# Gated DeltaNet in a one-core decoder step: the 32x32 block inverses in one tile, the keys' norm in the delta rows' factor

## The chip, the core and the metric

One core of one Trainium2 chip. The metric is the device time of one execution in microseconds (us), from the first instruction to the last and the little that lies around them; lower is better. The engines are named as the profile names them: PE (matmuls), PEld (its weight loads), DVE, ACT, POOL, and SP, which here does nothing but issue DMAs.

## What is computed

One inference step of a two-layer decoder in fp32: a gated DeltaNet layer with a SwiGLU block, then a sparse-attention layer with a second SwiGLU block. It handles a prompt of 512 positions and, beside it, 8 sampled sequences of 4 positions each. Only the DeltaNet layer (the first 410 us) is touched. It has 8 heads of width 128, and the part that matters is this:

```python
k = l2norm(k.reshape(B_, T, DN_HEADS, DN_HEAD_K))
...
kk = jnp.einsum('bnhid,bnhjd->bnhij', kc, kc)
A = jnp.where(strict, bc[..., :, None] * dec * kk, 0.0)
L = A + jnp.eye(C, dtype=A.dtype)
wv = lax.linalg.triangular_solve(L, bc[..., None] * vc, ...)
wk = lax.linalg.triangular_solve(L, (bc * eG)[..., None] * kc, ...)
aqk = dec * jnp.einsum('bnhid,bnhjd->bnhij', qc, kc)
kdec = jnp.exp(G[..., -1:] - G)[..., None] * kc
...
def step(S, xc):
    U = wv_n - jnp.einsum('bhik,bhkv->bhiv', wk_n, S)
    O = jnp.einsum('bhik,bhkv->bhiv', qg_n, S) + jnp.einsum('bhij,bhjv->bhiv', aqk_n, U)
    S = gl_n[..., None, None] * S + jnp.einsum('bhik,bhiv->bhkv', kdec_n, U)
```

So per head and chunk a unit triangular matrix L is inverted, and the state S is carried from chunk to chunk through the delta rows U. The kernel uses chunks of 128, four a head.

## The kernel before, in words

Every projection is a `gemm` (L171): for each of 8 slices of the model width three fp32r matmuls, the high parts (L177), the activations' low part (L178) and the weights' low part (L179), into a PSUM bank named mm. The weights come by DMA into `wraw` (three buffers), ACT rounds them to `whi` (L158, 128x1024) and POOL or DVE takes the rest into `wlo` (L159). Per head there are four projections: k, q and v, each followed by a causal convolution on ACT, DVE and POOL (`qkv`, L444), and the gate z (`zgate`, L679).

The heads' other work is written as small generators, each with a letter:

- K, `keys` (L511): decay factors, the keys' squared norms (transpose on PE at L525, squares on ACT at L526 into `ssk`), the matrix B = strict part of L into `BB` (L535). After heads 3 and 7 the 32x32 diagonal blocks of four heads go to DRAM (`scr`).
- S, `keys_done` with `key_cols` (L567): the per-row factors, among them `rk` (one over the keys' norm), `brk` = beta times rk, `kd` and `irk`.
- D, `diag_inverse` (L580): the 64 diagonal blocks of a group of four heads are inverted by substitution, one block a partition. It runs twice (D0, D1). The 32 rows of a block are held in two halves of 16 rows (a = 0, 1), D and N, each half in a buffer of its own; for step l from 31 to 1 DVE forms a product (L595) and a difference (L597), for both halves as long as l is over 16. Then ACT writes the transposes (L600), and the two results go to DRAM (`scn`).
- I, `inverse` (L606): loads the blocks into `XX` and `XT` and builds the 128x128 inverse by block products on PE.
- Q, `queries` (L645): keys times queries into PSUM, scaled by `rk` and the decays into `aq` (L657).
- V, `values` (L694): transposed values and keys, `Vs` and `Kd` (L706).
- `head` (L709): the chain over four chunks. For each: the state's share is taken off the values (L722, L723), the inverse is applied (L725), ACT multiplies by `brk` (L727) to give U, then come the state's update (L728, L732) and the output (L729, L735).
- s, `sample_ks` (L758): loads a sampled head's state in two buffers (256 KB each) and multiplies it (L770). P, `sample`: the sampled sequences' state updates, with two more such loads a head.

Buffers of 128x512 fp32 for all of this come from one pool, `hb()` (L439), of 32; `diag_inverse` takes five of them. PSUM banks named ch serve K and the heads' chains.

The order of the work is written as text: `DN_START` runs through, then each of four `DN_PAIRS` weaves the chains of two heads with other generators and a list of inverses, then `DN_TAIL`. But each engine's own order is not that of the text: the framework's scheduler (the kernel is built with it switched on) places the instructions of every engine by its own timing, and chooses which freed buffer a new tile takes. Each engine then runs its list in order and waits at the head of it.

Of the kernel before, what the change touches and what calls it, by code (L numbers as in the profile page):

```python
# [17 lines left out]
D = 1024  # L18
# [21 lines left out]
ESPAN = 640  # L40
HB = 32
DN_START = "k0 K0 q1 k2 k1 K2 v1 k3 K1 z0 K3 S0 k4 q0 K4 Q0 v0 V1 D0 k5 q3 s0 v4 z1 Q1 V0 K5 s3 k6 k7 I0 q2 v3 I1 K6 Q3 K7 s2 Y0 Q2 s1 v2 V3"
# [69 lines left out]
class Net:  # L112
# [206 lines left out]
    def deltanet(self, up, ctx):  # L319
# [10 lines left out]
        dn = ctx.enter_context(tc.tile_pool(name="dn", bufs=1))  # L330
        gc, bc, Gc, nG, eG, neG, GL, kd, gl, ssk, sB, rk, irk, brk, sq2 = [
            dn.tile([128, NG], F32, name=n) for n in
            ("gc", "bc", "Gc", "nG", "eG", "neG", "GL", "kd", "gl", "ssk", "sB", "rk", "irk", "brk", "sq2")]
        hist = dn.tile([128, 24, 24], F32, name="hist")
# [232 lines left out]
        def key_cols(s):  # L567
            g = slice(s * 17, s * 17 + 17)
            V.tensor_scalar(irk[:, g], ssk[:, g], EPS, None, op0=OP.add)
            self.rsqrt(rk[:, g], irk[:, g])  # L570
            V.tensor_tensor(irk[:, g], irk[:, g], rk[:, g], op=OP.mult)
            V.tensor_tensor(brk[:, g], bc[:, g], rk[:, g], op=OP.mult)
            S.activation(gl[:, g], GL[:, g], AF.Exp)
            V.tensor_tensor(kd[:, g], GL[:, g], nG[:, g], op=OP.add)
            S.activation(kd[:, g], kd[:, g], AF.Exp)
            V.tensor_tensor(kd[:, g], kd[:, g], rk[:, g], op=OP.mult)
            S.activation(eG[:, g], Gc[:, g], AF.Exp)
            V.tensor_scalar(neG[:, g], eG[:, g], -1.0, None, op0=OP.mult)

        def diag_inverse(g):  # L580

            D, N = [[hb()[0:64].rearrange("p (j i) -> p j i", i=32) for _ in range(2)] for _ in range(2)]
            tmp = hb()[0:64]
            rows = scr[4 * g:4 * g + 4].rearrange("h c b j i -> (h c b) j i")
            for a in range(2):
                self.dma(D[a], rows[:, 16 * a:16 * a + 16])
                G.memset(N[a], 0.0)
                G.memset(N[a].rearrange("p j i -> p (j i)")[:, 16 * a:512:33], 1.0)
            for l in range(31, 0, -1):
                n = 32 - l  # L590
                row = N[l // 16][:, l % 16:l % 16 + 1, l:32]
                for a in range(2 if l > 16 else 1):
                    m = min(l - 16 * a, 16)
                    t = tmp[:, 256 * a:256 * a + m * n].rearrange("p (j i) -> p j i", i=n)
                    V.tensor_tensor(t, D[a][:, 0:m, l:l + 1].to_broadcast([64, m, n]), row.to_broadcast([64, m, n]),  # L595
                                    op=OP.mult)
                    V.tensor_tensor(N[a][:, 0:m, l:32], N[a][:, 0:m, l:32], t, op=OP.subtract)  # L597
            for a in range(2):
                for b in range(2):
                    S.copy(D[a][:, :, 16 * b:16 * b + 16], N[b][:, :, 16 * a:16 * a + 16].rearrange("p j i -> p i j"))  # L600
            out = scn[g] = self.dr.tile([2, 4, NC, 4, 32, 32], F32, name=f"scn{g}")
            for t, o in ((N, out[0]), (D, out[1])):
                for a in range(2):
                    self.dma(o.rearrange("h c b j i -> (h c b) j i")[:, 16 * a:16 * a + 16], t[a])

# [39 lines left out]
        def queries(h):  # L645
# [7 lines left out]
            for c in range(NC):  # L653
                cs = slice(c * 128, (c + 1) * 128)
                T.matmul(ps[:, cs], lhsT=kT[h][:, cs], rhs=qT[h][:, cs], start=True, stop=True)
            for c in range(NC):
                V.scalar_tensor_tensor(aq[h][:, c], ps[:, c * 128:(c + 1) * 128], rk[:, col(h, c)],  # L657
                                       aq[h][:, c], op0=OP.mult, op1=OP.mult)
            yield
# [10 lines left out]
        def sample_query(s):  # L670
            ps = self.bank("ch")
            q2s = wk.tile([128, 128], F32, name="q2s", bufs=1)
            G.tensor_tensor(q2s, stk(qS, s), stk(qS, s), op=OP.mult)
            T.matmul(ps[:, 128:129], lhsT=q2s, rhs=ones[:, 0:1], start=True, stop=True)
            V.tensor_scalar(sq2[:, scol(s)], ps[:, 128:129], EPS, EPS * 128, op0=OP.add, op1=OP.mult)
            T.matmul(ps[:, 0:128], lhsT=stk(kS, s), rhs=stk(qS, s), start=True, stop=True)
            V.scalar_tensor_tensor(decs[:, s], ps[:, 0:128], rk[:, scol(s)], decs[:, s], op0=OP.mult, op1=OP.mult)

# [30 lines left out]
        def head(h):  # L709
# [5 lines left out]
            for c in range(NC):  # L715
# [10 lines left out]
                U = DX[:, 0, h % 2]  # L726
                S.mul(U, pa[:, 128:256], brk[:, cl])  # L727
                T.matmul(pa[:, 256:384], lhsT=Kd[h][:, c], rhs=U, start=True, stop=True)  # L728
# [49 lines left out]
        def sample_u(s):  # L778
# [7 lines left out]
            U = wk.tile([128, 128], F32, name="Us", bufs=1)  # L786
            S.mul(U, ps[:, 128:256], brk[:, cl])
            T.matmul(ps[:, 256:384], lhsT=decs[:, s], rhs=U, start=True, stop=True)
# [1018 lines left out]
```

## Time and profile before

| | |
|---|---|
| median of 3 runs | 1661.45 us (1659.9 to 1662.36) |
| profiled execution, its own time | 1664.61 us |
| its span, first to last instruction | 1662.4 us |
| mean granted TensorE clock | 0.985 |
| busy: PE / DVE / ACT / POOL | 1596.2 / 1059.6 / 710.8 / 562.3 us |

The page gives each engine's busy time, the chain of work that ended last, and the costliest groups of instructions. The trace behind it answers narrower questions: what an engine waited for in a stretch, what a stretch held, the instructions of one engine in order of time. Times in those answers are us from the start of the span.

### The profile page before, as it was taken

What the parts mean: (1) busy time and instruction counts of PE and PEld (TensorE: products, weight loads), DVE (VectorE), ACT (ScalarE), POOL (GpSimd) and SP (SyncE); (2) the same over time, 40 slices, a digit from 0 to 9 for tenths busy, and PEclk for the clock granted to TensorE, in tenths of its full rate; (3) what the DMA queues carried; (4) which work ended last, traced back from release to release, by engine and by line L of the source; (5) the groups of instructions that cost most, each with busy time, mean ns of one, the idle gap of its engine ahead of it and who ended that gap; (6) DMA issues with size and microseconds to landing.
All of it is one profiled execution on the core that took longest, in us unless ns stands there. A gap on an engine that the chain in (4) does not pass through costs nothing.

```text
span 1662.4 us, 32746 instructions
## 1 busy us (share of the span) xinstructions
PE 1596.2 (96%) x12527; PEld 1526.5 (92%) x12527; DVE 1059.6 (64%) x2543; ACT 710.8 (43%) x1796; POOL 562.3 (34%) x861
## 2 busy tenths in 40 slices
PE   8998899998989999999999999999999999999997
PEld 6998788886989999999999899877999999999997
DVE  4878779477557753555456598677875553355533
ACT  5554554554322222233332488688843232132233
POOL 2776546424356621100045476565520000000000
PEclk9999999999999999999999999999999999999999
DMA  6233512256556635354343533523133332334232
GB/s 195 77 79 84 118 36 67 69 162 210 145 134 150 161 104 120 99 159 137 106 136 87 139 93 88 174 65 120 45 94 104 102 106 79 108 90 127 77 88 81
DMA packets 289068, 183.36 MB, mean 110 GB/s; under 512 B 25183, under 2 KB 271784, under 8 KB 288784
## 3 DMA queue, kind: packets, MB, share of 16 engines
q1 hardware_dynamic: 286352, 172.88, 38.0%
q0 software_dynamic: 2560, 8.39, 1.4%
q8 instruction: 98, 1.61, 0.4%
q14 instruction: 58, 0.48, 0.1%
HBM read 159.33 MB, written 26.90 MB: 112 GB/s over the span
## 4 chain that ended last, share of the span: by engine, by line
PE 76%; DVE 10%; POOL 4%; DMA 4%; ACT 3%; issue 3%; SPq 1%; POOLq 0%; DVEq 0%; ACTq 0%
PE mm L179 15%; PE mm L177 15%; PE mm L178 15%; PE aux L177 5%; PE aux L179 5%; PE aux L178 5%; PE po L1629 2%; PE aux L1656 2%; DVE hb L595 2%; DVE hb L597 1%; SPq L155 1%; DVE wlo L159 1%; PE mm L1566 1%; PE mm L818 1%; PE mm L1567 1%
## 5 line engine op out<-in xcount | busy, mean ns | idle before, releaser
L177 PE MATMUL mm<-uh,whi 128*128 128x288 f32 (+2 forms) x1824 | 531.5, 293 | 5.3 <-DVE hb L689 1.7
L178 PE MATMUL mm<-ul,whi 128*128 128x288 f32 (+2 forms) x1824 | 530.4, 292 | 0.0
L179 PE MATMUL mm<-uh,wlo 128*128 128x288 f32 (+2 forms) x1824 | 524.0, 292 | 4.8 <-DVE wlo L159 4.8
L158 ACT CAST whi<-wraw 128x1024 fp32r<-128x1024 f32 (+5 forms) x231 | 216.1, 936 | 525.6 <-PE mm L178 412.7
L177 PEld LDWEIGHTS mm<-uh,whi 128*128 128x128 f32 (+1 forms) x1824 | 344.2, 189 | 8.6 <-DVE hb L689 2.1
L179 PEld LDWEIGHTS mm<-uh,wlo 128*128 128x128 f32 (+1 forms) x1824 | 341.1, 189 | 6.9 <-DVE wlo L159 6.0
L178 PEld LDWEIGHTS mm<-ul,whi 128*128 128x128 f32 (+1 forms) x1824 | 344.6, 189 | 1.5 <-issue 0.4
L159 DVE TENSOR_TENSOR wlo<-wraw,whi 128x1024 fp32r<-128x1024 f32 (+5 forms) x207 | 233.1, 1126 | 108.6 <-ACT whi L158 107.1
L179 PE MATMUL aux<-uh,wlo 128*128 128x288 f32 (+1 forms) x704 | 202.1, 287 | 1.0 <-DVE wlo L159 0.9
L177 PE MATMUL aux<-uh,whi 128*128 128x288 f32 (+1 forms) x704 | 203.0, 288 | 0.0
L178 PE MATMUL aux<-ul,whi 128*128 128x288 f32 (+1 forms) x704 | 202.7, 288 | 0.0
L177 PE MATMUL mm<-hh,whi 128*128 128x256 f32 (+1 forms) x704 | 202.1, 289 | 0.0
L178 PE MATMUL mm<-hl,whi 128*128 128x256 f32 (+1 forms) x704 | 201.4, 288 | 0.0
L179 PE MATMUL mm<-hh,wlo 128*128 128x256 f32 (+1 forms) x704 | 196.5, 288 | 0.0
L184 POOL TENSOR_TENSOR ycol<-yvar,nhalf 128x2 f32<-128x2 f32 (+1 forms) x2 | 1.6, 776 | 398.0 <-DVE yvar L1704 398.0
L179 PEld LDWEIGHTS aux<-uh,wlo 128*128 128x128 f32 x704 | 132.4, 188 | 1.4 <-DVE wlo L159 1.4
L178 PEld LDWEIGHTS mm<-hl,whi 128*128 128x128 f32 x704 | 132.7, 188 | 0.0
L177 PEld LDWEIGHTS mm<-hh,whi 128*128 128x128 f32 x704 | 132.6, 188 | 0.0
L178 PEld LDWEIGHTS aux<-ul,whi 128*128 128x128 f32 x704 | 132.6, 188 | 0.0
L177 PEld LDWEIGHTS aux<-uh,whi 128*128 128x128 f32 x704 | 132.3, 188 | 0.2 <-issue 0.2
L179 PEld LDWEIGHTS mm<-hh,wlo 128*128 128x128 f32 x704 | 129.6, 188 | 0.0
L957 DVE SCALAR_TENSOR_TENSOR fup<-aux,rstd 128x256 f32<-128x256 f32 x88 | 38.7, 440 | 125.5 <-PE aux L179 125.5
(535 smaller groups left out, 2961.1 us busy)
## 6 DMA issues: line engine op xcount, KB each, us to landing
wraw<-in_ffn_w_in_dram SPq DMA_DIRECT2D x88, 512.0 KB
wraw<-in_dn_w_in_dram SPq DMA_DIRECT2D x32, 512.0 KB
wraw<-in_ffn_w_out_dram SPq DMA_DIRECT2D x32, 384.0 KB
wraw<-in_ffn_w_out_dram SPq DMA_DIRECT2D x32, 320.0 KB
hb<-in_state_dn_S_dram SPq DMA_DIRECT2D x32, 256.0 KB
wraw<-in_nsa_w_kv_dram SPq DMA_DIRECT2D x12, 512.0 KB
bskew<-bscr SPq DMA_DIRECT2D x16, 320.0 KB
x<-xd SPq DMA_DIRECT2D x16, 272.0 KB
```

The costliest lines, as they stand in the source:

```text
L155: return self.nc.sync.dma_start(out, in_)
L158: self.S.copy(hi, src)
L159: (self.G if pool_lo else self.V).tensor_tensor(lo, src, hi.bitcast(F32), op=OP.subtract)
L177: self.T.matmul(ps, lhsT=hi[:, k, :], rhs=uh[:, cs], start=first and k == 0, stop=False)
L178: self.T.matmul(ps, lhsT=hi[:, k, :], rhs=ul[:, cs], start=False, stop=False)
L179: self.T.matmul(ps, lhsT=lo[:, k, :], rhs=uh[:, cs], start=False, stop=last and k == kc - 1)
L595: V.tensor_tensor(t, D[a][:, 0:m, l:l + 1].to_broadcast([64, m, n]), row.to_broadcast([64, m, n]), op=OP.mult)
L597: V.tensor_tensor(N[a][:, 0:m, l:32], N[a][:, 0:m, l:32], t, op=OP.subtract)
L818: T.matmul(ps, lhsT=Kh, rhs=um[q], start=True, stop=True)
L957: V.scalar_tensor_tensor(up, pu, 0.5, rstd[:, cs], op0=OP.mult, op1=OP.mult)
L1629: T.matmul(self.po, lhsT=self.VT[ty][:, kb, g], rhs=m[:, i:i + 2].rearrange("p e q -> p (e q)"), start=False, stop=last and kb > k0 and m ...
L1656: T.transpose(ps[:, i * 128:(i + 1) * 128], P[2 * pr + e][ty][:, a:a + 128], ident)
```

## The change

Four things change in the DeltaNet layer, and the pool of `hb()` buffers goes from 32 to 28.

1. `diag_inverse` holds the block's 32 rows in one tile each, `inv` [64, 32, 32], two buffers of 4 KB a partition that are its own; from `hb()` it takes only the scratch `tmp`. Each of the 31 steps is one product (L588 in the new file) and one difference (L590). One ACT copy (L591) in place of four writes the transposes. One DMA instead of two loads the blocks, and two instead of four store them.
2. `brk` is gone and `kd` no longer holds `rk`; U is multiplied by `sB` (beta over the squared norm).
3. So `aq` needs no factor by row: one product over 128x512 (L646) in place of four over 128x128.
4. The same in the sampled sequences' code.

```diff
-HB = 32
+HB = 28
...
-            V.tensor_tensor(brk[:, g], bc[:, g], rk[:, g], op=OP.mult)
...
-            V.tensor_tensor(kd[:, g], kd[:, g], rk[:, g], op=OP.mult)
...
-            D, N = [[hb()[0:64].rearrange("p (j i) -> p j i", i=32) for _ in range(2)] for _ in range(2)]
+            D, N = [wk.tile([64, 32, 32], F32, name="inv", bufs=2) for _ in range(2)]
             tmp = hb()[0:64]
-            rows = scr[4 * g:4 * g + 4].rearrange("h c b j i -> (h c b) j i")
-            for a in range(2):
-                self.dma(D[a], rows[:, 16 * a:16 * a + 16])
-                G.memset(N[a], 0.0)
-                G.memset(N[a].rearrange("p j i -> p (j i)")[:, 16 * a:512:33], 1.0)
+            self.dma(D, scr[4 * g:4 * g + 4].rearrange("h c b j i -> (h c b) j i"))
+            G.memset(N, 0.0)
+            G.memset(N.rearrange("p j i -> p (j i)")[:, 0:1024:33], 1.0)
             for l in range(31, 0, -1):
                 n = 32 - l
-                row = N[l // 16][:, l % 16:l % 16 + 1, l:32]
-                for a in range(2 if l > 16 else 1):
-                    m = min(l - 16 * a, 16)
-                    t = tmp[:, 256 * a:256 * a + m * n].rearrange("p (j i) -> p j i", i=n)
-                    V.tensor_tensor(t, D[a][:, 0:m, l:l + 1].to_broadcast([64, m, n]), row.to_broadcast([64, m, n]),
-                                    op=OP.mult)
-                    V.tensor_tensor(N[a][:, 0:m, l:32], N[a][:, 0:m, l:32], t, op=OP.subtract)
-            for a in range(2):
-                for b in range(2):
-                    S.copy(D[a][:, :, 16 * b:16 * b + 16], N[b][:, :, 16 * a:16 * a + 16].rearrange("p j i -> p i j"))
+                t = tmp[:, 0:l * n].rearrange("p (j i) -> p j i", i=n)
+                V.tensor_tensor(t, D[:, 0:l, l:l + 1].to_broadcast([64, l, n]), N[:, l:l + 1, l:32].to_broadcast([64, l, n]),
+                                op=OP.mult)
+                V.tensor_tensor(N[:, 0:l, l:32], N[:, 0:l, l:32], t, op=OP.subtract)
+            S.copy(D, N.rearrange("p j i -> p i j"))
...
             for t, o in ((N, out[0]), (D, out[1])):
-                for a in range(2):
-                    self.dma(o.rearrange("h c b j i -> (h c b) j i")[:, 16 * a:16 * a + 16], t[a])
+                self.dma(o.rearrange("h c b j i -> (h c b) j i"), t)
...
-            for c in range(NC):
-                V.scalar_tensor_tensor(aq[h][:, c], ps[:, c * 128:(c + 1) * 128], rk[:, col(h, c)],
-                                       aq[h][:, c], op0=OP.mult, op1=OP.mult)
+            V.tensor_tensor(aq[h], by_chunk(ps), aq[h], op=OP.mult)
...
-                S.mul(U, pa[:, 128:256], brk[:, cl])
+                S.mul(U, pa[:, 128:256], sB[:, cl])
```

The order texts are the same, but the engines' lists are not: the scheduler lays out the DeltaNet layer anew on every engine (the lists agree again after it). Three places are shown.

ACT, where the transposes of D0 are written. Before (L600 is the copy; `whi_3104` is the gate weight of head 6; L526 squares a chunk of head 4's or 5's keys, which PE's L525 in the same bank follows):

```order
L456 COPY pre_2413<-mm_2416 128x256
L492 COPY cso_2402<-ch_2400 108x128
L158 CAST whi_3104<-wraw_3102 128x1024
L456 COPY pre_2413<-mm_2442 128x256
L458 COPY pre_2413<-mm_2442 128x8x4
L600 COPY hb_1579<-hb_1581 64x16x16
L600 COPY hb_1580<-hb_1581 64x16x16
L526 ACTIVATE junk2_112,ssk_95<-ch_2532 128x128
L478 ACTIVATE cth_2380<-cy_2379 128x544
```

And after the change (L591 is the one copy, `whi_3007` the same gate weight):

```order
L456 COPY pre_2364<-mm_2367 128x256
L591 COPY inv_1573<-inv_1574 64x1024
L492 COPY cso_2353<-ch_2351 108x128
L158 CAST whi_3007<-wraw_3005 128x1024
L456 COPY pre_2364<-mm_2393 128x256
L458 COPY pre_2364<-mm_2393 128x8x4
L526 ACTIVATE junk2_111,ssk_95<-ch_2483 128x128
L478 ACTIVATE cth_2331<-cy_2330 128x544
```

The copy, which needs all of D0, now stands ahead of the weights' cast and two copies out of PSUM; L526 is behind it in both.

SP, around the states of sampled heads 2 and 1 (`hb<-in_state_dn_S_dram`, two loads a head). Before:

```order
L155 DMA wraw_3469<-in_dn_w_in_dram 128x8x128
L155 DMA hb_2607<-in_state_dn_S_dram 128x4x128
L155 DMA hb_2613<-in_state_dn_S_dram 128x4x128
L155 DMA hb_2647<-in_state_dn_S_dram 128x4x128
L155 DMA hb_2653<-in_state_dn_S_dram 128x4x128
L155 DMA XT_115<-scn0_1686 32x8x32
...
L155 DMA scr_411<-BB_116 32x16x32 x4
L155 DMA hb_2768<-scr_411 64x512
L155 DMA hb_2769<-scr_411 64x512
```

After:

```order
L155 DMA wraw_3369<-in_dn_w_in_dram 128x8x128
L155 DMA XT_114<-scn0_1642 32x8x32
...
L155 DMA scr_410<-BB_115 32x16x32 x4
L155 DMA inv_2713<-scr_410 64x1024
L155 DMA hb_2555<-in_state_dn_S_dram 128x4x128
L155 DMA hb_2561<-in_state_dn_S_dram 128x4x128
L155 DMA hb_2592<-in_state_dn_S_dram 128x4x128
L155 DMA hb_2598<-in_state_dn_S_dram 128x4x128
L155 DMA out_p_dn_S_dram<-DX_116 128x128 x2
```

The four loads have moved behind the stores and the load of the second group's blocks. Their buffers have changed as well: before, they were those that D0 had given up; now the first takes the buffer of head 0's keys, the second that of its `Vs`, the third that of head 1's keys, and the fourth the first's again.

PE, the chains of heads 0 and 1. Before, from the middle of them (`ch<-DX` and `ch<-hb,XX` are the chains; mm_3181 is the projection q of head 4; L770 stood 10 rows further up):

```order
L724 MATMUL ch_2921<-DX_117,hb_644 128x128
L725 MATMUL ch_2921<-hb_1562,XX_114 128x128
L722 MATMUL ch_2957<-DX_117,hb_529 128x128
L177 MATMUL mm_3181<-uh_134,whi_3174 128x256
L178 MATMUL mm_3181<-ul_135,whi_3174 128x256
L179 MATMUL mm_3181<-uh_134,wlo_3175 128x256
...
L724 MATMUL ch_2957<-DX_117,hb_1349 128x128
L699 MATMUL aux_2900<-ct_69,hb_2663 128x128 x4
L728 MATMUL ch_2921<-DX_117,hb_1563 128x128
```

After (L710, L712, L713, L716 and L717 are what L722, L724, L725, L728 and L729 were; L758 is what L770 was):

```order
L717 MATMUL ch_2874<-DX_116,hb_1095 128x128
L712 MATMUL ch_2899<-DX_116,hb_1346 128x128
L713 MATMUL ch_2899<-hb_1986,XX_113 128x128
L710 MATMUL ch_2912<-DX_116,hb_809 128x128
L758 MATMUL aux_2554<-hb_2555,km_112 64x128 x4
...
L717 MATMUL ch_2912<-DX_116,hb_1095 128x128
L549 MATMUL ch_2973<-kS_102 128x128
L758 MATMUL aux_2591<-hb_2592,km_112 64x128 x4
L758 MATMUL aux_2591<-hb_2598,km_112 64x128 x4
L177 MATMUL mm_3084<-uh_133,whi_3077 128x256
```

In the new list no projection stands between the first matmul of the two chains and the last L758; in the old one q of head 4 and z of head 5 began among them, 18 rows before the chains' third chunk was done. As many projections stand ahead of the chains in both.

## Rows read from the trace of the kernel before

**Rows 1.** The page: busy time by engine, and the chain that ended last.

```profile
PE 1596.2 (96%) x12527; PEld 1526.5 (92%) x12527; DVE 1059.6 (64%) x2543; ACT 710.8 (43%) x1796; POOL 562.3 (34%) x861
...
PE 76%; DVE 10%; POOL 4%; DMA 4%; ACT 3%; issue 3%; SPq 1%; POOLq 0%; DVEq 0%; ACTq 0%
```

**Rows 2.** Waits of PE, 100 to 410 us: total us, times, longest us.

```profile
PE ch L525 <- ACT junk L526: 9.5, 3, 4.6
...
PE aux L621 <- DMA XT<-scn: 1.7, 1, 1.7
```

**Rows 3.** Stretches: us, busy PE, PEld, DVE, ACT, POOL, granted clock, DMA share, GB/s.

```profile
142.40:149.20 6.80, 4.56 (x18) 4.27 (x19) 5.70 (x23) 4.16 (x12) 0.69 (x5) 0.50 0.25 71
183.30:186.70 3.40, 3.40 (x17) 3.40 (x16) 2.84 (x5) 0.92 (x5) 2.64 (x5) 0.50 0.58 115
202.00:214.00 12.00, 12.00 (x105) 9.19 (x106) 8.43 (x32) 6.89 (x21) 1.49 (x6) 1.00 0.37 84
```

**Rows 4.** The groups of DVE: line, tiles, count, busy us, mean ns, idle before.

```profile
L595 DVE TENSOR_TENSOR hb<-hb 64x112 f32<-64x112 f32 (+19 forms) x92 | 37.9, 436 | 1.8 <-POOL hb L588 0.6
L597 DVE TENSOR_TENSOR hb<-hb 64x112 f32<-64x112 f32 (+19 forms) x92 | 31.6, 365 | 0.6
L657 DVE SCALAR_TENSOR_TENSOR hb<-aux,rk,hb 128x128 f32<-128x128 f32 x32 | 9.0, 340 | 8.3 <-PE aux L655 8.2
...
L706 DVE TENSOR_TENSOR hb<-aux,kd 128x512 f32<-128x512 f32 x8 | 5.5, 681 | 2.3 <-PE aux L705 2.2
```

**Rows 5.** DVE in order of time, D0: start us, us; x2 is both halves.

```profile
128.67 0.47 DVE L595 TENSOR_TENSOR hb<-hb 64x96 f32<-64x96 f32 x2
129.07 0.44 DVE L597 TENSOR_TENSOR hb<-hb 64x96 f32<-64x96 f32 x2
129.54 0.45 DVE L595 TENSOR_TENSOR hb<-hb 64x112 f32<-64x112 f32 x2
...
147.55 0.48 DVE L595 TENSOR_TENSOR hb<-hb 64x240 f32<-64x240 f32 x2
147.98 0.48 DVE L597 TENSOR_TENSOR hb<-hb 64x240 f32<-64x240 f32 x2
148.50 0.42 DVE L595 TENSOR_TENSOR hb<-hb 64x256 f32<-64x256 f32 x1
148.95 0.42 DVE L597 TENSOR_TENSOR hb<-hb 64x256 f32<-64x256 f32 x1
149.41 0.42 DVE L595 TENSOR_TENSOR hb<-hb 64x255 f32<-64x255 f32 x1
...
174.22 0.31 DVE L597 TENSOR_TENSOR hb<-hb 64x156 f32<-64x156 f32 x1
```

**Rows 6.** POOL in order of time, 134 to 142 us.

```profile
134.42 2.77 POOL L451 COPY pre<-hist 128x24 f32<-128x24 f32 x1
137.14 4.17 POOL L477 TENSOR_TENSOR cy<-cy,cts 128x32 f32<-128x32 f32 x1
...
141.71 0.25 POOL L477 TENSOR_TENSOR cy<-cy,cts 128x32 f32<-128x32 f32 x1
```

**Rows 7.** ACT in order of time, 142 and 173 to 182 us; brackets: idle before.

```profile
142.65 0.66 ACT L478 ACTIVATE cth<-cy 128x544 f32<-128x544 f32 x1 [6.37 <-POOL cy L477]
...
173.84 1.05 ACT L158 CAST whi<-wraw 128x1024 fp32r<-128x1024 f32 x1
174.80 0.37 ACT L456 COPY pre<-mm 128x256 f32<-128x256 f32 x1
...
181.00 1.17 ACT L600 COPY hb<-hb 64x256 f32<-64x256 f32 x2 [5.74 <-DVE hb L597]
```

**Rows 8.** PE in order of time: two waits in the chains of heads 6 and 7.

```profile
379.38 0.49 PE L728 MATMUL ch<-DX,hb 128*128 128x128 f32 x2 [0.43 <-ACT DX L727]
...
382.49 0.49 PE L724 MATMUL ch<-DX,hb 128*128 128x128 f32 x2 [0.44 <-DVE hb L723]
```

**Rows 9.** The chain that ended last, a DMA of 285 to 293 us.

```profile
290.62 1.91 DMA XT<-scn
```

More of the change, by code (lines that the diff above doesn't have):

```diff
@@ L330, in deltanet @@
         dn = ctx.enter_context(tc.tile_pool(name="dn", bufs=1))
-        gc, bc, Gc, nG, eG, neG, GL, kd, gl, ssk, sB, rk, irk, brk, sq2 = [
+        gc, bc, Gc, nG, eG, neG, GL, kd, gl, ssk, sB, rk, irk, sq2 = [
             dn.tile([128, NG], F32, name=n) for n in
-            ("gc", "bc", "Gc", "nG", "eG", "neG", "GL", "kd", "gl", "ssk", "sB", "rk", "irk", "brk", "sq2")]
+            ("gc", "bc", "Gc", "nG", "eG", "neG", "GL", "kd", "gl", "ssk", "sB", "rk", "irk", "sq2")]
         hist = dn.tile([128, 24, 24], F32, name="hist")
@@ L676, in sample_query @@
             T.matmul(ps[:, 0:128], lhsT=stk(kS, s), rhs=stk(qS, s), start=True, stop=True)
-            V.scalar_tensor_tensor(decs[:, s], ps[:, 0:128], rk[:, scol(s)], decs[:, s], op0=OP.mult, op1=OP.mult)
+            V.tensor_tensor(decs[:, s], ps[:, 0:128], decs[:, s], op=OP.mult)
         def zgate(h):
@@ L786, in sample_u @@
             U = wk.tile([128, 128], F32, name="Us", bufs=1)
-            S.mul(U, ps[:, 128:256], brk[:, cl])
+            S.mul(U, ps[:, 128:256], sB[:, cl])
             T.matmul(ps[:, 256:384], lhsT=decs[:, s], rhs=U, start=True, stop=True)
```

## The prediction

> **What bounds the kernel now.** I read the page first, then PE's waits in the DeltaNet layer, then what DVE, POOL and ACT did before each of them. PE is busy for 96% of the span and holds 76% of the chain that ended last; DVE is busy for 64% and holds 10% [rows 1]. So a microsecond taken off DVE is worth nothing as such. It counts only where PE stands still because of it, and the waits tell where that is: L525 waited 9.5 us in all for the squares of L526, in three pieces, and L621 waited 1.7 us for a DMA [rows 2]. These places are all that the change can win from.
>
> The two large pieces have different causes. Stall A, 4.6 us long, ends at 144. ACT had been idle for 6.37 us because L478 needed POOL's L477 [rows 7], and POOL had taken 2.77 us for L451 and 4.17 us for L477, an operation that takes 0.25 us a moment later [rows 6]. At that time DVE ran D0's steps with hardly a gap. Stall B, some 4 us, ends at 182.5: ACT stood for 5.74 us at L600 until the last difference of D0, and L526 was next in its list [rows 7]. After each stall the granted clock was at 0.50 (1.2 in place of 2.4 GHz), for 6.8 us after A and for 3.4 us after B [rows 3]. Work at half clock takes double, so these cost about 3.4 and 1.7 us more. Between 202 and 214, while the chains of heads 0 and 1 ran, PE was busy for the whole 12 us and its clock was 1.00 [rows 3]; here the lists put other matmuls between the links.
>
> **D0 and D1 on DVE.** 60 instructions go, 15 products and 15 differences in each group (62 in place of 92 of each line remain together [rows 4]). What a pair costs is read from the starts. Early in D0, a product and a difference in two halves (96 elements in the longer) took 0.87 us from 128.67 to 129.54; a single one of the same 156 elements takes 0.31, and with the 0.03 us that the rows leave between neighbours 0.68 for two [rows 5]. So a step saves 0.19 us. At the last step with halves, 147.55 to 148.50 is 0.95 us against 0.90 or 0.91 for the next two with one instruction each: 0.05. I take the mean, 0.12 a step, so 1.8 us a group and 3.6 in all, with 0.05 and 0.19 (1.5 and 5.7 in all) as ends.
>
> The rows show a single 255-element product at 0.42 us, and its second half beside a first at hardly anything. [...]
>
> **The factor.** Four L657 at 0.340 become one product that reads PSUM at 128x512, for which L706 at 0.681 is the nearest row [rows 4]: up to 0.68 us a head, 5.4 in eight heads. It lies beside PE's projections and counts only for the two heads that stand inside D0's time, 1.4 us at most. The four small instructions on `kd` and `brk` and the memsets I put at nothing: they stand off the waits above, beside the same projections, and without that cover they would be shorter than a few of D0's steps.
>
> **Stall A.** Of the 15 steps with halves 11 end before it (the sixth and the last are in [rows 5]), so POOL gets free 11 x 0.12 = 1.3 us earlier: **-1.3**. The ends are 0 (POOL is held as long as before) and -8.0 (wait 4.6 and clock 3.4 gone). What the rows show is only that POOL's short operations stretch while DVE runs densely.
>
> **Stall B.** D0 ends earlier by 1.8 us for its steps and by about half of 1.4 for the factor, 2.5 in all; PE, having lost 1.3 us less at A, comes to the place 1.3 earlier too, so 1.2 is left. But the list of ACT is another one: behind D0's end stood 1.17 us of copies and then L526. Now come one copy of all 1024 elements, a cast (1.05), a copy out of PSUM (0.37) and two small ones, and only then L526 [rows 7]. The one copy lies between 1.17 and 2.34, which is what two and four old ones take; I take 1.7. Then L526 comes 1.7 + 1.05 + 0.37 - 1.17 = 1.95 us later after D0. Net 1.95 - 1.2, so **+0.7**, ends -5.7 (wait 4.0 and clock 1.7 gone) and +2 (a dear copy, a small saving).
>
> **D1.** It ends 1.8 us earlier, and its results go through one DMA each. The DMA that PE waits for lasts 1.91 us itself [rows 9] and stays; the wait of 1.7 is what can go. Against that D1's scratch buffer is free only after the second load of a sampled state has been used. I take **-1.2**, ends -3.4 (this wait, and a stretch at half clock like B's) and +1.
>
> **Heads 0 and 1.** This is what the change adds, by its lists. Their chains stand on PE with no projection between the links. Where that is so at the end of the layer, PE waits 0.43 us for ACT's U and 0.44 us for DVE's R in a chunk of two heads [rows 8]. That is 0.87 us for each of the three chunks that are bare: **+2.6**, ends 0 and 3.5 (all four chunks).
>
> The four loads of sampled states, issued long ahead before, now wait on SP for buffers that the chains themselves give up. The first can go when head 0's last L710 is done; five rows of the chain later PE wants it in L758. A short load took 1.91 us [rows 9], and five links of two matmuls take 1.1 us where PE never waits (105 matmuls in 12.00 us [rows 3]), so PE waits about a microsecond there and half of one more for the fourth load, which needs the first one's buffer: **+1.5**, ends 0 and 3.8 (two loads in series with nothing beside). Behind those loads SP holds the final states' stores and the next weights; the weights went out after the chains before, too, so nobody waits for them longer. The projections that used to stand between the links come later and cover PE there; that is no loss in PE's work, only in cover.
>
> **The sampled state updates (P).** With four buffers fewer, one of the first loads of P0 is held back until head 2 is finished. I take a quarter of a DMA, **+0.5**, ends 0 and 1.9.
>
> **Sum.** -1.3 + 0.7 - 1.2 + 2.6 + 1.5 + 0.5 = +2.8 us. On the profiled execution (1664.61, of which 1662.4 is span) that is 1667.4. This execution lies 3.2 us above the median of the three runs, so in their terms I say 1661.45 + 2.8 = **1664.3 us**. About 0.2%, 3.3 us, is what a measurement of this kernel can tell from no change, so this is no change, on its slower side.
>
> **Rival 1, faster: the stalls lose their slow clock.** If A and B shrink to half (-2.3 and -2.0), PE may keep its full clock behind them (-3.4 and -1.7). With D1's -1.2 against +4.6 from heads, loads and P that is -6.0, 1655.5 us. For it speaks that waits of 0.4 us in rows 8 came with none of this, and that A hangs on a handful of POOL instructions which a small shift frees. Against it: B's L526 has more ahead of it than before.
>
> **Rival 2, slower: the loads of the sampled states.** It is one mechanism at one place: L758 among the chains of heads 0 and 1 waits for loads that could only start when the chains let their buffers go. If both waits reach a whole DMA (3.8), the chains are bare in all four chunks (3.5) and the standstill is answered by 3.4 us at half clock as after B (1.7), that is +9.0; with the other terms (-1.3 + 0.7 - 1.2 + 0.5) it is +7.7, 1669.2 us. It decides from the point at which L758 waits about 3 us and the clock falls. For it speaks that nothing but chain links stands between release and use; against it, that the first pieces of each chain have other matmuls beside them still.
>
> **Rival 3, the same by another way.** DVE's saved work never reaches PE: A, B and D1 stay as they are, and the heads cost less than I take since ACT and DVE, with less to do, answer faster. It ends within 2 us of the old time and shares my forecast's class. That the change does not do what it says can be left out: the new lists show the 60 instructions gone.
>
> **Chances.** No change 0.36 (my sum and rival 3), slower 0.35 (rival 2, and milder forms of it, for which 0.5 us over my sum is enough), faster 0.29 (rival 1, or one of its two stalls gone alone). The likeliest case by itself spans 1660 to 1664.8. For 8 in 10 the range goes below rival 1 to 1652: both stalls wholly gone (-13.7) with D1's -1.2 and the +4.6 would be -10.3, 1651.2, and I stop just short of it. Above rival 2 it goes to 1672: the +9.0 with A and D1 giving nothing back and B and P as in the sum is +10.2, 1671.7. Beyond each end I leave one in ten.
>
> **What would show it.** In the new profile: 62 of L588 and of L590, together 50 us or less against 69.5 for L595 and L597; L646 eight times near 0.68. PE's wait of L525 for L526 at 7 to 9 us if my A and B hold, under 5 for rival 1, with fewer stretches at 0.50. New waits in the chains of heads 0 and 1: L716 on ACT, L713 on DVE, some 2.6 us, and L758 on a DMA, 1.5 us; over 3 us there and a half clock behind it is rival 2. My forecast is wrong if L525's waits vanish, or if L758's reach several microseconds.

## The result, and the profile after

The change made the kernel **slower by 1.15%**, by some 19 us: 1679.92 us in the median (1677.62 to 1681.64, 4 runs) against 1660.95 before (1659.9 to 1662.36, 4 runs); the ratio is 1.0115, with a 95% interval of 1.0099 to 1.013. I had said no change, 1664.3 us, and a range that ended at 1672. The profiled execution took 1678.22 us, its span 1676.5. The two profiled executions differ by 13.6 us (1678.22 less 1664.61), since that of the kernel before was slower than its median and that of the kernel after a little faster; so the traces can place some 14 of the 19 us.

The page of the kernel after, engines and chain (against [rows 1]):

```profile
PE 1604.2 (96%) x12527; PEld 1534.0 (92%) x12527; DVE 1057.2 (63%) x2455; ACT 711.7 (42%) x1790; POOL 560.0 (33%) x857
...
PE 73%; DVE 10%; DMA 6%; POOL 5%; issue 3%; ACT 3%; SPq 1%; POOLq 0%; DVEq 0%; ACTq 0%
```

DVE has 88 instructions fewer and is busy 2.4 us less; what has grown in the chain is DMA, from 4% to 6%. The groups of DVE and ACT that the change touches, kernel after (against [rows 4]; L591 is the copy on ACT):

```profile
L590 DVE TENSOR_TENSOR inv<-inv,hb 64x31 f32<-64x31 f32 (+15 forms) x62 | 31.2, 503 | 1.3
L588 DVE TENSOR_TENSOR hb<-inv 64x31 f32<-64x31 f32 (+15 forms) x62 | 30.1, 485 | 1.3
L646 DVE TENSOR_TENSOR hb<-aux,hb 128x512 f32<-128x512 f32 x8 | 5.5, 688 | 10.4 <-PE aux L645 10.4
...
L591 ACT COPY inv<-inv 64x1024 f32<-64x1024 f32 x2 | 4.0, 2001 | 5.7 <-DVE inv L590 5.7
```

The instructions did what they were meant to do: 61.3 us in place of 69.5 for the inverses, 5.5 in place of 9.0 for the queries' factor. The new time is elsewhere. What PE waited for from 60 to 450 us in the kernel after (total, times, longest; against [rows 2]):

```profile
PE ch L525 <- ACT junk L526: 4.2, 2, 4.0
PE aux L758 <- DMA hb<-in_state_dn_S_dram: 3.9, 2, 2.8
PE mm L177 <- ACT pre L456: 3.7, 1, 3.7
PE ch L533 <- ACT cso L492: 3.4, 1, 3.4
...
PE mm L789 <- DVE B L787: 3.3, 1, 3.3
```

Stalls A and B are still there (L525 behind L526 at 4.0, and L533 behind L492, which now stands right behind D0's copy on ACT, at 3.4). Two are new: L758 for a sampled head's state, and a projection for L456, the copy that empties its PSUM bank. To see where the time goes by place, I take from both traces the start of the same projection matmul (lines L177 to L179; there are 9,696 and both kernels run them in the same order of projections) and subtract. Positive is later than before:

```
projection matmul no.      720    960   1008   1152   1296   1440   1776   last
before, at us            136.2  187.1  214.1  247.9  279.2  305.1  422.2 1650.8
after, later by us        -1.1   -1.1   +8.5   +5.5   -3.1  +10.2  +14.6  +14.1
```

Up to no. 960 the two are alike. The +8.5 at no. 1008 is mostly the moved order (projections that stood between the chains' links now follow them), and at no. 1296 the kernel is even 3.1 ahead. Then, from no. 1296 to 1440, **it falls back by 13 us in one place**, some 276 to 315 us of its own time, and ends the DeltaNet layer 14.6 behind.

Part of this is moved work too: 234 matmuls of PE start between these two numbers, 198 before the change, and in the stretch ahead of it 180 in place of 218. The whole stretch from no. 960 to 1440 holds nearly the same work in both kernels (columns as in [rows 3]; the kernel before first):

```profile
187.10:305.10 118.00, 109.79 (x925) 101.63 (x923) 93.03 (x261) 61.16 (x174) 66.43 (x105) 0.99 0.32 81
186.00:315.30 129.30, 116.47 (x928) 106.27 (x927) 87.85 (x218) 62.07 (x171) 63.75 (x105) 0.95 0.28 73
```

It takes 11.3 us longer. PE stands still for 12.8 us in it in place of 8.2, and it is longer at half clock, by the mean granted clock of 0.95 in place of 0.99.

DVE in that place, kernel after, in order of time (start, duration; brackets: idle before):

```profile
273.27 2.42 DVE L590 TENSOR_TENSOR inv<-inv,hb 64x31 f32<-64x31 f32 x1
289.02 0.69 DVE L694 TENSOR_TENSOR hb<-aux,kd 128x512 f32<-128x512 f32 x1 [13.33 <-PE aux L758]
...
292.72 1.52 DVE L479 SCALAR_TENSOR_TENSOR hb<-cth,cy 128x512 f32<-128x512 f32 x1 [0.89 <-PE aux L741]
...
295.70 3.85 DVE L470 SCALAR_TENSOR_TENSOR cy<-pre,cw,cy 128x512 f32<-128x512 f32 x5
```

DVE does nothing for 13.33 us after D1's last difference. Next in its list is L694, head 4's `Kd`, and what it waits for is not its PSUM operand but PE's L758: the buffer that it writes was last read there. The operand is not early, though: L693, which makes it, is done at 288.1, only 0.9 us ahead of the start of L694. SP and PE in the same place, two views of the kernel after:

```profile
275.72 0.49 SPq L155 DMA_DIRECT2D scn<-inv  x1
276.30 0.55 SPq L155 DMA_DIRECT2D hb<-in_state_dn_S_dram  x1
...
283.36 0.40 SPq L155 DMA_DIRECT2D hb<-in_state_dn_S_dram  x1
```

```profile
279.91 1.12 PE L758 MATMUL aux<-hb,km 128*64 128x128 f32 x8 [2.79 <-DMA hb<-in_state_dn_S_dram]
...
287.52 0.60 PE L693 MATMUL aux<-ct,hb 128*128 128x128 f32 x4
288.32 0.66 PE L758 MATMUL aux<-hb,km 128*64 128x128 f32 x8
```

The kernel before issued both loads long ahead of D1's end (its last difference ended at 286.0):

```profile
258.96 6.15 SPq L155 DMA_DIRECT2D hb<-in_state_dn_S_dram  x2
```

By the addresses in the built program, which no view here prints, D1's scratch `tmp`, the first load of sampled head 4, its second load and head 4's `Kd` are, one after the other, **the same buffer**. The trace bears out the last three: ahead of L694, DVE's queue waits on the semaphores that tell of the landing of the first load (at 279.9) and of the second (at 286.3). So they can only follow each other: D1 ends at 275.7, the load starts at 276.3 and PE has it at 279.9; the second starts at 283.4 and is used at 288.3; `Kd` is written at 289.0. Not all of the 13.33 us is the buffer: the second load stands on SP until 283.4 behind loads of inverted blocks, though PE was done with the first at 281.0, and L693 and the second L758 come late in PE's own list. These lists were laid out together with the buffers, and the trace does not part the two. Behind L694 on DVE five L470 have piled up (two convolutions), ACT stands behind those, and PE's next projection waits 3.7 us for its PSUM bank.

The clock makes it dearer. Stretches of the kernel after (us, busy PE, PEld, DVE, ACT, POOL, granted clock, DMA share, GB/s; against [rows 3]):

```profile
142.50:149.30 6.80, 5.75 (x24) 5.51 (x23) 6.29 (x18) 2.22 (x7) 0.00 (x0) 0.50 0.02 6
180.10:183.50 3.40, 3.40 (x18) 3.40 (x17) 2.32 (x3) 2.50 (x10) 3.40 (x4) 0.51 0.54 103
...
279.00:285.90 6.90, 5.99 (x32) 5.63 (x32) 0.00 (x0) 2.23 (x9) 2.54 (x2) 0.51 0.53 129
299.50:302.90 3.40, 2.81 (x11) 2.81 (x12) 1.94 (x5) 3.38 (x12) 2.56 (x10) 0.50 0.00 0
...
203.00:219.00 16.00, 13.91 (x97) 10.49 (x99) 7.07 (x25) 8.26 (x28) 0.50 (x2) 1.00 0.45 115
276.00:300.00 24.00, 16.39 (x115) 14.86 (x113) 8.26 (x12) 9.40 (x21) 11.54 (x21) 0.85 0.49 125
```

A and B are followed by the half clock as before. New are 6.9 us of it behind L758's wait and 3.4 us behind L456's, some 4 us of lost speed. That is an estimate: projection matmuls of 128x288 start 0.240 us apart at 0.50 (300.50 to 302.66) and 0.133 us apart at 1.00 (303.06 to 303.98), so of the 8.8 us that PE was busy in the two stretches 3.9 are the half clock's. Between 276 and 300 PE is busy for 16.39 of 24 us. The chains of heads 0 and 1 (203 to 219) keep the full clock, at 13.91 of 16 us. The kernel before had in the same two stretches:

```profile
203.00:219.00 16.00, 16.00 (x139) 13.38 (x138) 9.42 (x31) 8.22 (x28) 1.52 (x6) 1.00 0.23 51
276.00:300.00 24.00, 21.23 (x175) 20.62 (x176) 17.61 (x32) 13.80 (x33) 17.12 (x28) 1.00 0.44 106
```

### The profile page after: what moved, and what is told of

Same layout as the page of the kernel before. It is cut to its first block, busy times and chain, and to the rows that moved or that the text cites. A ratio compares the mean times of both kernels' runs of the same rounds, so it can differ in the third digit from the quotient of the medians.

```text
span 1676.5 us, 32647 instructions
## 1 busy us (share of the span) xinstructions
PE 1604.2 (96%) x12527; PEld 1534.0 (92%) x12527; DVE 1057.2 (63%) x2455; ACT 711.7 (42%) x1790; POOL 560.0 (33%) x857
## 4 chain that ended last, share of the span: by engine, by line
PE 73%; DVE 10%; DMA 6%; POOL 5%; issue 3%; ACT 3%; SPq 1%; POOLq 0%; DVEq 0%; ACTq 0%
PE mm L177 15%; PE mm L179 14%; PE mm L178 14%; PE aux L177 5%; PE aux L179 5%; PE aux L178 5%; PE po L1617 2%; PE aux L1644 2%; DVE inv L590 1%; DVE hb L588 1%; DVE wlo L159 1%; PE mm L1554 1%; DVE cy L470 1%; PE mm L1555 1%; DMA wraw<-in_ffn_w_in_dram 1%
## 5 line engine op out<-in xcount | busy, mean ns | idle before, releaser
L177 PE MATMUL mm<-uh,whi 128*128 128x288 f32 (+2 forms) x1824 | 533.1, 294 | 10.7 <-ACT pre L456 3.7
L179 PE MATMUL mm<-uh,wlo 128*128 128x288 f32 (+2 forms) x1824 | 525.3, 293 | 6.9 <-DVE wlo L159 6.9
L177 PEld LDWEIGHTS mm<-uh,whi 128*128 128x128 f32 (+1 forms) x1824 | 345.8, 190 | 15.3 <-DVE hb L677 3.9
L179 PEld LDWEIGHTS mm<-uh,wlo 128*128 128x128 f32 (+1 forms) x1824 | 342.9, 190 | 8.9 <-DVE wlo L159 7.8
L159 DVE TENSOR_TENSOR wlo<-wraw,whi 128x1024 fp32r<-128x1024 f32 (+5 forms) x207 | 237.0, 1145 | 109.3 <-ACT whi L158 107.8
L179 PE MATMUL aux<-uh,wlo 128*128 128x288 f32 (+1 forms) x704 | 203.0, 288 | 2.6 <-DVE wlo L159 2.6
L177 PE MATMUL aux<-uh,whi 128*128 128x288 f32 (+1 forms) x704 | 203.7, 289 | 0.0
L177 PE MATMUL mm<-hh,whi 128*128 128x256 f32 (+1 forms) x704 | 202.1, 289 | 0.0
L179 PE MATMUL mm<-hh,wlo 128*128 128x256 f32 (+1 forms) x704 | 196.5, 288 | 0.0
L179 PEld LDWEIGHTS aux<-uh,wlo 128*128 128x128 f32 x704 | 133.0, 189 | 3.4 <-DVE wlo L159 3.4
L177 PEld LDWEIGHTS aux<-uh,whi 128*128 128x128 f32 x704 | 133.0, 189 | 0.2 <-issue 0.2
L177 PEld LDWEIGHTS mm<-hh,whi 128*128 128x128 f32 x704 | 132.6, 188 | 0.0
L179 PEld LDWEIGHTS mm<-hh,wlo 128*128 128x128 f32 x704 | 129.7, 188 | 0.0
```

The source lines that it names most:

```text
L159: (self.G if pool_lo else self.V).tensor_tensor(lo, src, hi.bitcast(F32), op=OP.subtract)
L177: self.T.matmul(ps, lhsT=hi[:, k, :], rhs=uh[:, cs], start=first and k == 0, stop=False)
L179: self.T.matmul(ps, lhsT=lo[:, k, :], rhs=uh[:, cs], start=False, stop=last and k == kc - 1)
```

## The experiments

Three theories were set against each other first. P: the pool, 28 buffers in place of 32. M: the merged tile, whose results leave only when all 31 steps are done. F: the factor. Later P was split: P1, what the short pool starves is the loads at the chains of heads 0 and 1; P2, it acts further on. The ratios below are to the kernel before on the same chip, which ran there at medians of 1665.5 to 1666.8 us; times named in an expectation were set from the earlier 1661, so the ratios are what to compare.

**e1_hb28**, the number alone:

```diff
-HB = 32
+HB = 28
```

> The kernel before with one number changed: 28 buffers in place of 32; nothing of the inverses or of the factor. Its lists already show the bare chains of heads 0 and 1 and the late loads of sampled states. If the missing buffers make the loss (theory P): 1672 to 1682 us, with PE waiting for state loads beside the chains and less cover around 270 to 340 us. If the merged tile makes it (theory M): 1658 to 1666 us, or the few us that bare chains cost alone, up to 1668. If the factor makes it (theory F): as before, 1659 to 1664.

1689.0 us, ratio 1.0147 (1.0121 to 1.0172): P, with more than I forecast, and at least as much as the whole change loses. But it is not the change's loss at the change's place: with halves, D0 and D1 take five of the 28 buffers, and e1's trace loses nearly all its time between no. 960 and 1152 (in the table of lags further down). **e2_factor**, the other end: the kernel before with the diff's lines on `brk`, `kd`, `aq`, `decs` and U alone.

> The kernel before with only the keys' norm moved into the delta rows' factor (32 buffers, halves kept). Theories P and M: 1655 to 1663 us, the saved DVE work being under PE; its chains have projections between the links as before. Theory F: over 1670 us. L646 once a head near 0.68 us in all three.

1667.75 us, ratio 1.0013 (0.9995 to 1.003): no difference that can be told. F is out, and the DVE time that the factor saves is worth nothing, as forecast. **e3_merge** takes those lines out of the change and leaves the merged tile with its 28 buffers:

> The merged inverse tile with its 28 buffers, and the keys' norm left where it was. Theories P and M: 1674 to 1685 us, as the whole change. Theory F: 1660 to 1668 us.

1681.48 us, ratio 1.011 (1.0085 to 1.0136): as the change. Since e1 shares the 28 buffers and differs in the merged tile, the merged tile costs nothing that shows beside them; it is nearer to giving something back (1.011 against 1.0147), which fits that it takes one buffer from the pool where the halves take five.

**e4_store_queue** asks whether it was the order on SP, where the load stands behind the store that waits for D1:

```diff
-                self.dma(o.rearrange("h c b j i -> (h c b) j i"), t)
+                self.nc.scalar.dma_start(o.rearrange("h c b j i -> (h c b) j i"), t)
```

> The whole change, but the two stores of the inverted blocks are issued from ACT's queue, so that on SP no load of a sampled state stands behind a store that waits for D1's last step. If that order on SP makes the loss (a part of theory M: 2.8 us of waiting at 277 us and 3.4 us for the half clock behind it, and the standstill of DVE): 1668 to 1674 us with no wait of PE for the fifth pair of loads. Theory P: 1675 to 1684 us, since the buffers of the loads come free no sooner.

1681.73 us, ratio 1.0113 (1.0087 to 1.014). What PE waited for between 200 and 345 us in e4, and DVE's wait in it:

```profile
PE aux L758 <- DMA hb<-in_state_dn_S_dram: 4.2, 3, 2.8
PE mm L177 <- ACT pre L456: 3.2, 1, 3.2
```

```profile
285.22 0.69 DVE L694 TENSOR_TENSOR hb<-aux,kd 128x512 f32<-128x512 f32 x1 [11.76 <-PE aux L693]
```

The first wait is the same, and by the addresses the same four users share one buffer. With the store out of the way the first load still cannot go before D1's end: SP waits 8.0 us for L590, and the load starts at 273.53, as D1 ends. So the store ahead of it was not what held it. What e4 leaves open is SP's share in the second load, which goes out at 281.08 behind loads that wait for the same stores, though PE was done with the first buffer at 277.9; and L694 waits at the end for its operand, L693. That the merged tile's late results make the loss (M) is not borne out by e1, e3 or e4.

**e7_hb30** and **e8_hb29** ask how much is too few. The edit is that of e1 with 30 and 29.

> The kernel before with 30 buffers. Its lists keep projections between the links of heads 0 and 1, and the four loads stand where they stood; the fifth sampled head is later. P1: 1660 to 1667 us, as with 32. P2: a step on the way to 28, 1670 to 1680 us.

> The kernel before with 29 buffers; the second of the four loads is late among the chains in its lists, the chains themselves have projections between them. P1: 1663 to 1670 us. P2: 1675 to 1685 us, between 30 and 28 buffers.

1683.5 us, 1.0101 (1.008 to 1.0123), and 1690.24 us, 1.0148 (1.0119 to 1.0177). Two buffers fewer already cost 1%, though the chains of heads 0 and 1 have their projections and their loads as before. So P1 is not the whole of it, and the second place shows the same pile behind another wait. SP and DVE in e7, in order of time:

```profile
283.35 1.76 SPq L155 DMA_DIRECT2D scn<-hb  x3
285.61 1.00 SPq L155 DMA_DIRECT2D hb<-in_state_dn_S_dram  x2
```

```profile
290.83 0.28 DVE L775 TENSOR_TENSOR KSs<-aux,KSs 32x128 f32<-32x128 f32 x1 [5.41 <-ACT KSs L774]
...
296.72 3.89 DVE L470 SCALAR_TENSOR_TENSOR cy<-pre,cw,cy 128x512 f32<-128x512 f32 x5 [0.20 <-issue]
```

By their semaphores the two loads, of the fifth sampled head, wait for the landing of D1's first two stores: they take buffers in which D1's results lay. DVE waits for the copy of their product (L774), and five L470 pile up behind it.

**e5_shared_s** mends the first place in the changed kernel: the two inverse tiles, idle between D0 and D1, take the states of sampled heads 2 and 1.

```diff
-            D, N = [wk.tile([64, 32, 32], F32, name="inv", bufs=2) for _ in range(2)]
+            D, N = [big()[0:64] for _ in range(2)]
...
+            if h in (1, 2):
+                two = big().rearrange("p j i -> p (j i)")
...
-                s0 = hb().rearrange("p (b v) -> p b v", v=128)
+                s0 = (two[:, 512 * q:512 * q + 512] if h in (1, 2) else hb()).rearrange("p (b v) -> p b v", v=128)
```

(`big()` gives one of two tiles of [128, 32, 32], the former `inv`.)

> The whole change, but the states of sampled heads 2 and 1 are loaded into the two inverse tiles (free between D0 and D1) in place of four of the 28 buffers. The lists show projections between the links of heads 0 and 1 again. If the late loads of these two heads and the bare chains are the loss (theory P1: what the 28 buffers starve is this place): 1660 to 1667 us. If the shortage acts all along, on the projections of heads 4 to 7 that find no buffer for their output (theory P2): 1672 to 1680 us, some 5 us less than the change at the chains and the rest still lost between 230 and 340 us.

1674.3 us, ratio 1.0054 (1.0022 to 1.0086): about half of the loss is gone, and half is left, in the second place. **e6_shared_all** gives the sampled updates' loads the same tiles.

> As e5_shared_s, and the sampled state updates load their states into the inverse tiles as well, one tile for the two loads of a head. P1: as e5_shared_s within 3 us, 1658 to 1668. P2: up to 3 us faster than e5_shared_s, since the buffers are then free for the outputs of projections at 340 to 400 us, but still over 1670 us.

1687.81 us, ratio 1.0116 (1.0097 to 1.0135), against both theories. I read it as the same queue for buffers once more, with two tiles for eight pairs of loads, between 340 and 420 us: there PE waits 2.8 us for a load (L763) and 4.7 us for states in the inverse tiles (L813). Its lag at projection matmul no. 1776 is 21.5 us, of which 14 came after no. 1535.

**e9_finish_early** mends the second place, by the order text alone. F0 and F1 give back the gates and outputs of heads 0 and 1, four buffers:

```diff
-            ("S1 z6 C0 q4 z5 Q4 v6 s4 V4 v5 F0 q5 F1 V5 I4 v7 q6 q7 V7 V6 Q5 I5 Q7 z7 z2 Q6 z4 P0", "", 118),
+            ("S1 z6 C0 F0 F1 q4 z5 Q4 v6 s4 V4 v5 q5 V5 I4 v7 q6 q7 V7 V6 Q5 I5 Q7 z7 z2 Q6 z4 P0", "", 118),
```

> The whole change with one edit in the order text: F0 and F1, which give back two buffers a head (the head's output and its gate), stand right behind C0 and not behind the projections v5 and q5. The lists show the loads of the fifth sampled head and the projections of head 5 earlier. If the outputs of the projections wait for these buffers (theory P2, and the pile of five L470 in a row behind a DVE that idles 12 us is that wait): 1664 to 1672 us, with the loss at the chains of heads 0 and 1 left. If the loss after 270 us is only the late loads' (theory P1): within 4 us of the change, 1675 to 1684 us.

1671.56 us, ratio 1.0037 (1.0018 to 1.0055). By the program's lists the loads of sampled head 4 now take two buffers that F0 and F1 gave back, which no view prints. SP and DVE in e9, in order of time:

```profile
257.47 1.72 SPq L155 DMA_DIRECT2D hb<-in_state_dn_S_dram  x2
268.13 0.37 SPq L155 DMA_DIRECT2D wraw<-in_dn_w_in_dram  x1
277.45 2.59 SPq L155 DMA_DIRECT2D scn<-inv  x2
```

```profile
275.14 2.28 DVE L590 TENSOR_TENSOR inv<-inv,hb 64x31 f32<-64x31 f32 x1
277.46 0.69 DVE L694 TENSOR_TENSOR hb<-aux,kd 128x512 f32<-128x512 f32 x1
278.06 0.68 DVE L479 SCALAR_TENSOR_TENSOR hb<-cth,cy 128x512 f32<-128x512 f32 x1
```

Both loads go out 20 us ahead of D1's store, and L694 follows D1 at once: the 13.33 us are gone. **e10_finish_early_shared** has both mends.

> e9_finish_early, and the states of sampled heads 2 and 1 in the inverse tiles as in e5_shared_s. P2: both places mended, so the time of the kernel before or a little under it: 1654 to 1664 us. P1: as e5_shared_s, 1668 to 1676 us.

1667.47 us, ratio 1.0005 (0.9989 to 1.0022): all of the loss is gone. Its waits of PE between 200 and 300 us hold neither L456 nor a load:

```profile
PE aux L690 <- DVE hb L482: 2.0, 1, 2.0
PE aux L631 <- DVE XT L625: 1.6, 2, 0.9
PE ch L565 <- DVE B L564: 1.6, 1, 1.6
PE aux L621 <- DVE Y L616: 0.2, 1, 0.2
```

**e11_before_finish_early** is the control: the same text in the kernel before.

> The control: the same edit of the order text in the kernel before, with its 32 buffers, halves and factor. P2: 32 buffers are enough for the projections, so the edit is worth 0 to 4 us here: 1657 to 1667 us. If the edit is worth 8 us or more here too, it mends something other than the missing buffers.

1668.93 us, ratio 1.0024 (1.0008 to 1.004). With 32 buffers and halves the edit gains nothing, it loses a little, where I had expected 0 to 4 us of gain; so in e9 and e10 it mends what the short pool broke. The lags of the kernels of interest, in us, along the same projection matmuls:

```
projection matmul no.       960   1008   1152   1296   1440   1776   last
after                      -1.1   +8.5   +5.5   -3.1  +10.2  +14.6  +14.1
e1  28 buffers only        -4.6   +9.6  +22.1  +19.0  +18.9  +23.8  +26.5
e2  factor only            -3.0   -3.3   -3.3   -3.4   -4.8   +0.7   +3.9
e5  loads of s2, s1        -2.5   -2.4   -4.2   -9.7   +3.9   +9.2   +9.2
e7  30 buffers only        -2.2   -2.6   +4.9   -1.0  +12.7  +15.4  +14.2
e8  29 buffers only        -1.0   -0.4  +11.8   +9.6  +17.1  +22.8  +23.1
e9  F0, F1 early           -1.0   +8.7   +5.6   +1.0   +2.8   +7.8   +8.5
e10 both                   -2.6   -2.4   -4.3   -6.2   -4.3   +0.1   +2.9
e11 before, F0, F1 early   -1.5   -1.5   -1.5   -2.6   -0.7   +6.3   +9.7
```

Each row is one execution, and steps of 2 or 3 us are not to be read. e5 takes away the step at no. 1008, e9 the step from 1296 to 1440, e10 both. e10 and e2 are 4 to 5 us ahead of the kernel before until no. 1440 and lose that again before the layer ends. But from no. 1440 to 1776 every row loses 2.7 to 7 us, also e2 and e11 with their 32 buffers; so what is lost there is not the pool's, and the pool's part of the 14.6 us is nearer to 10. With fewer buffers and halves (e1, e8) half of the loss or more comes ahead of no. 1152.

**e12_third_finish** was meant to keep it, with F2 ahead of the chains of heads 4 and 5:

```diff
-            ("o0 I6 I7", "", 12),
-            ("F2 o1 z3 C1 F3 s7 o2 o3 w0 p2 F4 s5 s6 F5 Y1 P1", "", 33))
+            ("F2 o0 I6 I7", "", 12),
+            ("o1 z3 C1 F3 s7 o2 o3 w0 p2 F4 s5 s6 F5 Y1 P1", "", 33))
```

> A version meant to beat both: e10_finish_early_shared, and F2 moved ahead into the third pair's list, so that head 2's two buffers come back before the chains of heads 4 and 5. P2 (what the 28 buffers cost is cover that comes too late): 0 to 5 us under e10_finish_early_shared, 1656 to 1664 us, since the lists show two fewer bare links there. If the buffers are enough by then: within 2 us of e10_finish_early_shared.

1664.97 us, ratio 1.0004 (0.999 to 1.0019). It does not beat e10 or the kernel before by anything that can be measured. The merged tile with all 32 buffers was not tried: its two tiles take just the 8 KB a partition that the four buffers gave up. So the tile beside an undiminished pool stands untested.

## Why the prediction was wrong, step by step

**Stalls A and B** agree with the forecast as far as one trace can tell: -0.6 us together by the sum, -1.1 at no. 960 (e3 and e4, with the same inverses, read -2.3 and -3.3 there). B came out by another way, though: D0 ended 4.1 us earlier (176.9 for 181.0), not 2.5; the copy L591 took 2.0 us where I took 1.7; and PE waited not at L525 for L526 but at L533 for L492, which stands right behind that copy. So the sign that I gave for rival 1, L525's waits under 5 us, showed (4.2) without rival 1. Nor does work at half clock take double: in the kernel before, projection matmuls of 128x288 start 0.240 us apart at 0.50 (183.52 to 186.40) and 0.133 us apart at 1.00 (191.48 to 193.21), 1.8 times. In columns that is 1.2 a ns at 0.50 and 2.2 at 1.00, where the prediction has 1.2 and 2.4 GHz. With PE busy for 4.56 us of the stretch after A and for 3.40 after B [rows 3], the half clock cost an estimated 2.0 and 1.5 us, not 3.4 and 1.7. **The DVE prices** held where they can be read: L646 0.688 for 0.681; the inverses gave back 8.2 us of busy time by the groups (61.3 us are left, where I had set 50 or less as a sign, which does not follow from my own saving of 3.6), but those hold single instructions of over 2 us in both kernels (before, L595 of 64x156 at 171.81 took 2.38 us, with a mean of 0.436; after, L588 of 64x220 at 161.03 took 2.46, with a mean of 0.485), so this is no clean measure of the 3.6. As forecast, none of it reached the time; e2 shows that for the factor.

**Heads 0 and 1** were forecast at +4.1, 2.6 for the chains and 1.5 for the loads, with the right place and cause. The waits of PE there read 1.1 us for the first load and 0.7 for U in four pieces, less than I took, and e5, which mends this place, ends 5.4 us (14.6 less 9.2 at no. 1776) ahead of the change; the rest may be the cover that I put at nothing. PE's waits from 203 to 219 us, kernel after:

```profile
PE aux L758 <- DMA hb<-in_state_dn_S_dram: 1.1, 1, 1.1
PE ch L716 <- ACT DX L715: 0.7, 4, 0.2
```

The half clock that rival 2 added did not come (203 to 219 us at 1.00).

**The step that failed is the price of the pool.** I wrote of the loads that "the projections that used to stand between the links come later and cover PE there; that is no loss in PE's work, only in cover", gave the four missing buffers +0.5 at the sampled updates, and, for D1, set -1.2 with the remark that its scratch comes free late. I priced what comes into a buffer ahead of D1 and not what comes after. In the kernel after, three more users stand in line for D1's scratch; DVE stands for 13.33 us behind D1, and PE loses 2.79 us and 3.7 us in waits and runs 10.3 us at half clock behind them. D1 itself ended 10.3 us earlier than before (275.7 for 286.0), and the wait that I took off for it went, but what stood behind it cost more. The term for D1 should have been about +6 in place of -1.2: e9, which breaks the line by giving the loads other buffers, is 7.4 us ahead of the change at no. 1440 (10.2 less 2.8) and 6.8 at no. 1776. Of rival 2 the mechanism was right, loads that could only start when a buffer was let go, but at the wrong pair of loads: the fifth sampled head's, not the third's and second's.

The range failed with it. Each of my terms was one wait with its neighbours; none held the case that fewer buffers delay several waits in a row, and e7 says that even two fewer, with the four loads in place, cost 1%.

What is shown: that a shorter pool alone loses as much as the change (e1, e7, e8), though in the kernel with halves partly at other places; that the factor does not make the loss (e2, e3), nor the merged tile once the two places are mended (e10), nor the store ahead of the first load on SP (e4); and that mending two places gives all of it back (e5, e9, e10). What is argued: how the line for D1's scratch makes PE's waits, for e9 breaks it by an order text that lays out every engine's list anew, so the buffer and the lists are not parted. What stays open is why every other kernel is 2.7 us or more slower than the kernel before from no. 1440 to 1776; with e2 and e11 among them it is not the pool. That the last heads' chains find no more projections to cover them is a guess; e12 tried to move that and did not.

## What to carry to other kernels

Buffers of a pool that a scheduler hands out are a resource like an engine: when a change takes some away to make a tile of its own, find for every late user of the pool who had its buffer before, and who gets it next, and price the whole line. Memory set aside for something that runs a quarter of the time (D0 and D1, some 105 of the layer's 410 us) is paid for all the time; letting the idle tiles hold other data and giving buffers back earlier in the order each undid a half of the loss or more, and both together all of it. And busy time saved on DVE bought nothing that shows, in three kernels that saved it: e2 (5.5 us for 9.0 at the queries' factor; ratio 1.0013), e10 (the same, and 60.2 us for 69.5 at the inverses; 1.0005) and e12 (e10's instructions in another order; 1.0004).

## What was not expected of the hardware

The merged copy on ACT, 64x1024 with a transposing pattern, took 2.00 us, hardly less than four of 64x256 in pairs (2 x 1.17 us by [rows 7]), so merging them saved some 0.3 us. And the granted clock went down 0.9 and 0.6 us before the ends of single waits of 2.79 and 3.7 us (to 0.51 and 0.50) but stayed at 1.00 in the chains of heads 0 and 1, where PE stood still for 2.1 of 16 us in pieces of 1.12 us and less.
